# Value projections of both mixers over 512 weight columns at a time, in a two-layer encoder on one core

## The chip, the cores and the metric

The kernel runs on one core of one Trainium2 chip. The metric is the device time of one execution in microseconds (us), taken as the median of several runs. Within a core TensorE (PE in the tables; PEld is its weight load, which runs beside its matmuls), VectorE (DVE), ScalarE (ACT) and GpSimd (POOL) each work through a queue of their own in order, and wait for each other by semaphores. SyncE (SP) issues the weight transfers.

## The reference, cut to what matters

512 tokens of width 1024 pass two layers. Layer 0 joins a gated linear recurrence in both directions (4 heads of 128) with a latent attention (4 heads); layer 1 is a differential attention with 8 heads. Each is followed by a gated hidden layer of width 2816. The values that the change touches are plain projections of the normed input `h`:

```
z = h @ w_in                                       # layer 0, columns split
q_h, f_fw, f_bw, i_h, g_h, cq, ckv, kr = jnp.split(z, AB_SPLITS, axis=-1)
v = heads(i_h)                                     # 4 heads x 128 = columns 1536..2047
o_a = hgrn2_scan(q, k_fw, v, lf_fw) + flip(hgrn2_scan(flip(q), flip(k_bw), flip(v), flip(lf_bw)))
...
q, k, v = jnp.split(h @ w_in, 3, axis=-1)          # layer 1
v = v.reshape(bsz, s, DIFF_HEADS, 2 * DIFF_HEAD_DIM)   # 8 heads x 128 = columns 2048..3071
```

## The kernel before, in words

Every projection is computed in three matmuls per block of 128 input rows (`mm3`, L245): both operands are split into a high and a low part, and high x high, high x low and low x high are added up in one PSUM bank. The weights come in pieces of 128 x 1024 numbers in the order of a written list (`weight_plan`, L48): SP loads a piece (`_load`), ACT rounds it to its high part `whi`, DVE subtracts to get `wlo` (`_split`, L227 and L228). Two raw pieces and four split pieces fit at a time; a split piece is free again when TensorE has read it for the last time.

There are two forms of projection. `features` has the weights as the stationary operand and streams all 512 tokens, 256 columns (two heads) to a call, so its matmuls are 128x512; in the trace they read `mm<-oph,whi`. `values` (L293) has the tokens as the stationary operand and streams weight columns, since its result must stand with tokens on the partitions: before, a call covers 256 columns (two heads), so each matmul is 128x256 (`mm<-whi,oph`), and four token blocks x 8 input blocks x 3 make 96 of them. There are two such calls in layer 0 (at the end of `gates(0)` and `gates(1)`, L571) and four in layer 1 (at the end of `diff_inputs`, L989).

The order of TensorE's work is as the program writes it. Generators are woven: `weave` gives each thread a step count, and the thread with the smallest share done goes next. In layer 0, `gates(0)` runs by itself; then `gates(1)` is woven with the scans of heads 0 and 1 (`hgrn`, L566), and the latent projections with the scans of heads 2 and 3. A scan begins with `kk`, a sum on POOL (L575), and the matmuls `lv<-q,kk` (L579) that read it; then come seven levels, each with copies on ACT (L595, L597), products on DVE (`merge`, L649), a product on POOL (L652) and a matmul (L587). The other engines' queues are set by a scheduler, which puts `kk` behind the gate product `g` (L558) on POOL.

In layer 1 the first pair of heads gets its inputs alone (`need(0)`); then the inputs of the other pairs are woven with `diff_heads`, a pipeline over 32 units (8 heads x 4 token blocks): scores `sc`, softmax, transposition `pt`, product with the values `o`, and at a head's end a transposition back `ot`. What is left of the heads is woven with the first half of the output projection `c_out`; the last `ot` stands in its second half. Eight PSUM banks are shared by all.

Of the kernel before, what the change touches and what calls it, by code (L numbers as in the profile page):

```python
# [20 lines left out]
AF = mybir.ActivationFunctionType  # L21
# [26 lines left out]
def weight_plan():  # L48
    plan = []
    for p in range(2):  # L50
        for base in (512, 1024, 0, 2048, 1536):
            plan += [("ab_in", k, 4, base + 256 * p, 256) for k in (0, 4)]
    for c in (2560, 2816, 3072):
        plan += [("ab_in", k, 4, c, 256) for k in (0, 4)]
    plan += [("uq", k, 1, 0, 768) for k in range(3)]
    plan += [("ukv", k, 1, 0, 1024) for k in range(2)]
    for k in (0, 4):
        plan += [("ab_out", k, 4, 256 * j, 256) for j in range(4)]
    plan += ffn_plan(0)
    for hp in range(4):  # L60
        for base in (0, 1024, 2048):
            plan += [("c_in", k, 4, base + 256 * hp, 256) for k in (0, 4)]
    for k in (0, 4):
        plan += [("c_out", k, 4, 256 * j, 256) for j in range(4)]
    plan += ffn_plan(1)
    return plan
# [57 lines left out]
class Kernel:  # L124
# [108 lines left out]
    def weight(self, *key, ahead=2):  # L233
# [7 lines left out]
        hi, lo = self.splits.pop(i)  # L241
        return tuple(t[:, :kn * cn].rearrange("p (k n) -> p k n", k=kn) for t in (hi, lo))


    def mm3(self, ps, lhs, rhs, first, last):  # L245
        mm = self.nc.tensor.matmul
# [46 lines left out]
    def values(self, w, cols, xop, r):  # L293


        V = self.s4("v")
        wt = [self.weight(w, k, 4, cols, 256, ahead=a) for k, a in ((0, 2), (4, 1))]
        for b2 in range(2):
            ps = self.bank()
            for i in range(2):  # L300
                b = 2 * b2 + i
                for k in range(8):
                    self.mm3(ps[:, 256 * i:256 * i + 256], tuple(v[:, b * 128:(b + 1) * 128] for v in xop(k)),
                             tuple(v[:, k % 4, :] for v in wt[k // 4]), k == 0, k == 7)
                    if k % 4 == 3 and (i, k) != (1, 7):
                        yield
            for i in range(2):
                b = 2 * b2 + i
                self.nc.scalar.activation(V[:, b2, 256 * i:256 * i + 256], ps[:, 256 * i:256 * i + 256], AF.Copy,
                                          scale=r[:, b:b + 1])  # L310
            yield
        return V


# [218 lines left out]
    def gates(self, p, xg, st):  # L533

        nc = self.nc
        st += [dict(F=self.s4("F"), QK=self.s8("QK")) for _ in range(2)]
        for d, base in ((0, 512), (1, 1024)):
            def forget(i, ps):
                h = 2 * p + i
                if self.R is None:  # L540
                    self.R = self.spread(self.r)
                z = self.s2("z")
                nc.vector.tensor_mul(z[:], ps[:], self.R[:])
                sp = self.s2("sp")
                nc.scalar.activation(sp[:], z[:], AF.Sigmoid)
                nc.scalar.activation(z[:], z[:], AF.Sigmoid, scale=-1.0)
                f, k = st[i]["F"][:, d, :], st[i]["QK"][:, 3 * d, :]
                nc.vector.tensor_scalar(f, sp[:], self.oml[:, d, h:h + 1], self.lb[:, d, h:h + 1], ALU.mult, ALU.add)
                nc.vector.tensor_scalar_mul(k, z[:], self.omlc[:, d, h:h + 1])

            yield from self.features("ab_in", base + 256 * p, FULL, xg, forget)
        for nm, base in (("q", 0), ("g", 2048)):
            def silu(i, ps):
                z = self.s2("z")
                nc.vector.tensor_mul(z[:], ps[:], self.R[:])
                s = self.s2(nm)
                nc.scalar.activation(s[:], z[:], AF.Sigmoid)
                nc.gpsimd.tensor_mul(s[:], z[:], s[:])  # L558
                st[i][nm] = s
                if nm == "q":  # L560
                    nc.vector.tensor_mul(st[i]["QK"][:, 2, :], s[:], st[i]["F"][:, 0, :])
                    nc.vector.tensor_mul(st[i]["QK"][:, 1, :], s[:], st[i]["F"][:, 1, :])

            yield from self.features("ab_in", base + 256 * p, FULL, xg, silu)
        st[0]["V"] = st[1]["V"] = yield from self.values("ab_in", 1536 + 256 * p, xg, self.r)

    def hgrn(self, h, st, oa):


        nc = self.nc  # L570
        F, QK, V, q, g = (st[n] for n in ("F", "QK", "V", "q", "g"))  # L571
        AT = self.s8("AT")
        diag = ap(AT, 0, [[640, 4], [1, 128]])
        kk = self.s2("kk")
# [1 line left out]
        ps = self.bank("lv")  # L576
# [39 lines left out]
        for half, (ks, qs) in enumerate(((0, 2), (3, 1))):  # L616
            ps = self.bank("lv")
            t0 = 256 * (1 - half)
            for i in range(2):
                b = 2 * half + i  # L620
# [2 lines left out]
            nc.scalar.copy(AT[:, 2 * half:2 * half + 2, t0:t0 + 256],  # L623
                           ps[:].rearrange("p (b t) -> p b t", b=2))
        yield
        po = self.bank("o")
        for t in range(NB):
            for s in range(NB):
                c0 = 256 * (s % 2) + 128 * (h % 2)
# [342 lines left out]
    def diff_inputs(self, hp, xg, stats, st):  # L972

        nc = self.nc
        st += [dict(qk=self.s8("qk", F32R), kl=[self.s2("kl", F32R) for _ in range(2)]) for _ in range(2)]
        for j, base in enumerate((0, 1024)):
            todo = [] if self.R is not None else [lambda: setattr(self, "r", self.rms(stats[0], D))]

            def turn(i, ps):
                if self.R is None:  # L980
                    self.R = self.spread(self.r)
                    self.rcos, self.rsin = self.s2("rcos"), self.s2("rsin")
                    nc.vector.tensor_mul(self.rcos[:], self.R[:], self.cos)
# [5 lines left out]
        st[0]["V"] = st[1]["V"] = yield from self.values("c_in", 2048 + 256 * hp, xg, self.r)  # L989

    def diff_heads(self, sts, op, need):

# [64 lines left out]
    def layer0(self):  # L1057
        op = self.operand()
        lat = {}
        s0, s1 = [], []  # L1060
        self.R = None
        self.setup()
        xg = self.operand()
# [21 lines left out]
        next(work)  # L1085
        self.late_constants()
        drain(work)
        weave((self.gates(1, xg, s1), 42), (self.hgrn(0, s0[0], op), 13), (self.hgrn(1, s0[1], op), 17))
        scans = [self.hgrn(2, s1[0], op), self.hgrn(3, s1[1], op)]
        weave((self.latents(self.R, xg, lat), 32), (scans[0], 11), (scans[1], 11), lead=True)  # L1090
        weave((self.mla_heads(lat, op), 92), (scans[0], 27), (scans[1], 27),
# [5 lines left out]
    def layer1(self, xg, stats):  # L1097
# [5 lines left out]
        def inputs():  # L1103
            for hp in range(4):
                yield from self.diff_inputs(hp, xg, stats, st[hp])
                done.append(hp)
                yield

# [6 lines left out]
        need(0)  # L1115
        self.ended = []
        heads = self.diff_heads(st, op, need)
        weave((work, 72), (heads, 95), lead=True)
        while len(self.ended) < 4:
            next(heads)  # L1120
        weave((self.projection("c_out", [(0, 4)], op), 10), (heads, 25))
# [65 lines left out]
```

## Time and profile before

| | us |
|---|---|
| median of 3 runs (range) | 1326.63 (1326.47 to 1327.24) |
| profiled execution, its own time | 1326.59 |
| its span, first to last instruction | 1324.8 |
| TensorE busy | 1306.2 |
| DVE busy | 759.8 |
| ACT busy | 539.1 |
| POOL busy | 159.5 |

The profile gives one execution. Durations of matmuls overlap, since TensorE begins one while the one before drains; what a matmul costs is the distance between two starts, and that is read from the timeline. What a line of `mm3` does in one call or another is told apart by the names and shapes.

### The profile page before, as it was taken

Reading aid. Unit: us, or ns where it says so; the run is one execution under the profiler, and the core shown is the slowest. Engines: PE = TensorE matmul, PEld = TensorE weight load, DVE = VectorE, ACT = ScalarE, POOL = GpSimd, SP = SyncE. Lnnn points to the kernel's source line nnn. Section 1 sums busy time; section 2 is a strip of 40 time slices with the busy share of each in tenths; the row PEclk is TensorE's granted clock in tenths of the full one; section 3 lists DMA queues with packets and bytes.
Section 4 is the critical chain, followed back from the end, with each engine's and each line's share of the span. In section 5 each row is a group of like instructions: output and inputs, shape, how many; then the busy total and the mean of one; then the engine's idle time right before and its main releaser. Section 6 shows DMA issues by size and latency. Waiting matters only on the chain. (4 is left out here: it accounts for less than half of the span.)

```text
span 1324.8 us, 16816 instructions
## 1 busy us (share of the span) xinstructions
PE 1306.2 (99%) x6666; PEld 1111.7 (84%) x6666; DVE 759.8 (57%) x1196; ACT 539.1 (41%) x938; POOL 159.5 (12%) x147
## 2 busy tenths in 40 slices
PE   7999999999999999999999999999999999999997
PEld 6888988888888888888888889888788888888886
DVE  5677499645444344434467888887745534433454
ACT  6454464744322222212253566665433212322332
POOL 0322232002000000000034223120300000000002
PEclk9999999999999999999999999999999999999999
DMA  6321331112232333233232221221232233223321
GB/s 211 112 79 49 87 93 65 48 33 80 88 102 97 96 96 95 95 96 95 87 105 80 80 65 49 64 65 49 80 95 96 96 98 103 98 98 95 95 96 64
DMA packets 106675, 115.15 MB, mean 87 GB/s; under 512 B 6826, under 2 KB 98660, under 8 KB 106596
## 3 DMA queue, kind: packets, MB, share of 16 engines
q1 hardware_dynamic: 105268, 112.10, 26.8%
q10 hardware_dynamic: 1328, 1.97, 0.4%
q8 instruction: 52, 0.85, 0.3%
q14 instruction: 27, 0.22, 0.1%
HBM read 111.97 MB, written 2.10 MB: 86 GB/s over the span
## 5 line engine op out<-in xcount | busy, mean ns | idle before, releaser
L247 PE MATMUL mm<-oph,whi 128*128 128x512 f32 (+1 forms) x1320 | 520.4, 394 | 1.6 <-ACT whi L227 1.6
L249 PE MATMUL mm<-oph,wlo 128*128 128x512 f32 (+1 forms) x1320 | 513.4, 389 | 0.0
L248 PE MATMUL mm<-opl,whi 128*128 128x512 f32 (+1 forms) x1320 | 513.0, 389 | 0.0
L228 DVE TENSOR_TENSOR wlo<-raw,whi 128x1024 fp32r<-128x1024 f32 (+1 forms) x190 | 228.5, 1203 | 287.4 <-ACT whi L227 286.5
L227 ACT CAST whi<-raw 128x1024 fp32r<-128x1024 f32 (+1 forms) x190 | 195.0, 1027 | 400.8 <-PE mm L248 242.0
L249 PEld LDWEIGHTS mm<-oph,wlo 128*128 128x128 f32 x1320 | 248.4, 188 | 51.5 <-DVE wlo L228 0.2
L247 PEld LDWEIGHTS mm<-oph,whi 128*128 128x128 f32 x1320 | 248.7, 188 | 50.3 <-ACT whi L227 2.0
L248 PEld LDWEIGHTS mm<-opl,whi 128*128 128x128 f32 x1320 | 248.8, 188 | 48.9 <-DVE opl L256 0.5
L247 PE MATMUL mm<-whi,oph 128*128 128x256 f32 (+1 forms) x374 | 125.2, 335 | 0.0
L249 PE MATMUL mm<-whi,opl 128*128 128x256 f32 (+1 forms) x374 | 123.8, 331 | 0.0
L248 PE MATMUL mm<-wlo,oph 128*128 128x256 f32 (+1 forms) x374 | 123.8, 331 | 0.0
L348 POOL TENSOR_TENSOR sq<-sq,sq 128x512 f32<-128x512 f32 x24 | 34.9, 1454 | 459.8 <-ACT sq L354 459.6
L248 PEld LDWEIGHTS mm<-wlo,oph 128*128 128x128 f32 x374 | 71.0, 190 | 6.9
L247 PEld LDWEIGHTS mm<-whi,oph 128*128 128x128 f32 x374 | 70.9, 190 | 6.9
L249 PEld LDWEIGHTS mm<-whi,opl 128*128 128x128 f32 x374 | 70.9, 190 | 6.6
L704 ACT ACTIVATE p<-sc,mx 128x512 f32<-128x512 f32 x80 | 55.1, 691 | 45.2 <-DVE mx L702 40.7
L880 DVE TENSOR_TENSOR z<-mm,R 128x512 f32<-128x512 f32 x44 | 30.4, 692 | 59.7 <-PE mm L249 55.5
L255 ACT CAST oph<-u 128x512 fp32r<-128x512 f32 x44 | 27.4, 622 | 87.3 <-DVE u L887 87.3
L701 DVE TENSOR_REDUCE mx<-sc 128x1 f32<-128x512 f32 x80 | 53.2, 681 | 16.1 <-PE sc L843 13.6
L519 DVE TENSOR_TENSOR xT<-xT,mm 128x512 f32<-128x512 f32 x56 | 38.4, 685 | 34.4 <-PE mm L249 34.4
L722 PEld LDWEIGHTS o<-v,pt 128*128 128x128 f32 x384 | 49.4, 191 | 3.1
L722 PE MATMUL o<-v,pt 128*128 128x128 f32 x384 | 50.6, 274 | 0.0
(193 smaller groups left out, 1297.5 us busy)
## 6 DMA issues: line engine op xcount, KB each, us to landing
raw<-in_ffn_w_gate_dram SPq DMA_DIRECT2D x44, 512.0 KB, 3.6
raw<-in_ffn_w_up_dram SPq DMA_DIRECT2D x44, 512.0 KB, 3.6
raw<-in_ffn_w_down_dram SPq DMA_DIRECT2D x42, 512.0 KB, 3.4
raw<-in_ab_w_in_dram SPq DMA_DIRECT2D x24, 512.0 KB, 3.6
raw<-in_c_w_in_dram SPq DMA_DIRECT2D x24, 512.0 KB, 3.6
xs<-in_x_dram SPq DMA_DIRECT2D x8, 512.0 KB, 6.1
raw<-in_ab_w_out_dram SPq DMA_DIRECT2D x8, 512.0 KB, 3.4
raw<-in_c_w_out_dram SPq DMA_DIRECT2D x8, 512.0 KB, 3.4
```

The source lines that it names most:

```text
L227: self.nc.scalar.copy(h, r)
L228: self.nc.vector.tensor_sub(l, r, h.bitcast(F32))
L247: mm(ps, lhsT=lhs[0], rhs=rhs[0], start=first, stop=False)
L248: mm(ps, lhsT=lhs[0], rhs=rhs[1], start=False, stop=False)
L249: mm(ps, lhsT=lhs[1], rhs=rhs[0], start=False, stop=last)
L255: nc.scalar.copy(hi, src)
L348: self.nc.gpsimd.tensor_add(acc[0][:], acc[0][:], s[:])
L519: nc.vector.tensor_add(self.x(j), self.x(j), ps)
L701: nc.vector.reduce_max(m[:], ps, axis=AX.X)
L704: nc.scalar.activation(p[:], ps, AF.Exp, bias=m[:], scale=scale, accum_out=l)
L722: self.nc.tensor.matmul(po[:, tb * 128:(tb + 1) * 128], lhsT=pt[:, s * 128:(s + 1) * 128], rhs=V[:, s // 2, c:c + 128], start=s == 0, stop ...
L880: nc.vector.tensor_mul(z[:], ps[:], self.R[:])
```

## The change

`values` now takes 512 columns (four heads) in one call. The six calls become three: one in layer 0, columns 1536 to 2047, and two in layer 1. A weight piece holds two input blocks x 512 columns where it held four x 256, so there are as many pieces and bytes as before (12 pieces). A call goes twice over its four pieces, for two token blocks each time, and holds two PSUM banks during each pass; it yields 16 times, each time after six matmuls of 128x512. `prefetch` splits the pieces that come after the call during the second pass.

In layer 0 the call no longer stands in `gates`: `scan_values` runs ahead of `gates(1)`, in the weave with the scans of heads 0 and 1, and a scan looks its values up only at its last product. In layer 1 the call follows the inputs of head pairs 0 and 2.

```diff
 def weight_plan():
     plan = []
     for p in range(2):
-        for base in (512, 1024, 0, 2048, 1536):
+        for base in (512, 1024, 0, 2048):
             plan += [("ab_in", k, 4, base + 256 * p, 256) for k in (0, 4)]
+        if p == 0:
+            plan += [("ab_in", k, 2, 1536, 512) for k in range(0, 8, 2)]
...
+    def prefetch(self, n):
+
+        while self.n_split <= min(self.n_used + n - 1, len(self.plan) - 1):
+            self._split()
...
     def values(self, w, cols, xop, r):
...
-        V = self.s4("v")
-        wt = [self.weight(w, k, 4, cols, 256, ahead=a) for k, a in ((0, 2), (4, 1))]
+        V = [self.s4("v"), self.s4("v")]
+        wt = []
         for b2 in range(2):
-            ps = self.bank()
-            for i in range(2):
-                b = 2 * b2 + i
-                for k in range(8):
-                    self.mm3(ps[:, 256 * i:256 * i + 256], tuple(v[:, b * 128:(b + 1) * 128] for v in xop(k)),
-                             tuple(v[:, k % 4, :] for v in wt[k // 4]), k == 0, k == 7)
-                    if k % 4 == 3 and (i, k) != (1, 7):
-                        yield
...
+            pss = [self.bank(), self.bank()]
+            for j in range(4):
+                if b2 == 0:
+                    wt.append(self.weight(w, 2 * j, 2, cols, 512, ahead=min(2, 3 - j)))
+                else:
+                    self.prefetch(j - 1)
+                for i in range(2):
+                    b = 2 * b2 + i
+                    for k in (2 * j, 2 * j + 1):
+                        self.mm3(pss[i][:], tuple(v[:, b * 128:(b + 1) * 128] for v in xop(k)),
+                                 tuple(v[:, k % 2, :] for v in wt[j]), k == 0, k == 7)
+                    if j == 3:
+                        for p in range(2):
+                            self.nc.scalar.activation(V[p][:, b2, 256 * i:256 * i + 256],
+                                                      pss[i][:, 256 * p:256 * p + 256], AF.Copy, scale=r[:, b:b + 1])
+                    yield
         return V
...
-        st[0]["V"] = st[1]["V"] = yield from self.values("ab_in", 1536 + 256 * p, xg, self.r)
+
+    def scan_values(self, xg, *sts):
+
+        V = yield from self.values("ab_in", 1536, xg, self.r)
+        for st, v in zip(sts, V):
+            for s in st:
+                s["V"] = v
...
-        weave((self.gates(1, xg, s1), 42), (self.hgrn(0, s0[0], op), 13), (self.hgrn(1, s0[1], op), 17))
+        weave((self.chain(self.scan_values(xg, s0, s1), self.gates(1, xg, s1)), 48),
+              (self.hgrn(0, s0[0], op), 13), (self.hgrn(1, s0[1], op), 17))
...
                 yield from self.diff_inputs(hp, xg, stats, st[hp])
+                if hp % 2 == 0:
+                    V = yield from self.values("c_in", 2048 + 256 * hp, xg, self.r)
+                for s in st[hp]:
+                    s["V"] = V[hp % 2]
                 done.append(hp)
                 yield
...
-        weave((work, 72), (heads, 95), lead=True)
+        weave((work, 68), (heads, 95), lead=True)
```

The first place is TensorE's queue where the scans of heads 0 and 1 begin. Before, the 96 value matmuls stand between the last gate feature and the features with which the scans are woven; these are the rows from the last value matmul on (`lv<-q,kk` are the scans' first matmuls):

```order
L249 MATMUL mm_629<-whi_531,opl_235 128x256
L247 MATMUL mm_684<-oph_108,whi_572 128x512
L248 MATMUL mm_684<-opl_109,whi_572 128x512
L249 MATMUL mm_684<-oph_108,wlo_573 128x512
L247 MATMUL mm_684<-oph_108,whi_572 128x512
L248 MATMUL mm_684<-opl_109,whi_572 128x512
L249 MATMUL mm_684<-oph_108,wlo_573 128x512
L579 MATMUL lv_707<-q_475,kk_705 128x128 x4
L579 MATMUL lv_716<-q_494,kk_714 128x128 x4
L247 MATMUL mm_684<-oph_120,whi_572 128x512
```

With the change the rows from the last gate feature (`mm_500`) on are these:

```order
L258 MATMUL mm_500<-oph_234,wlo_456 128x512
L256 MATMUL mm_573<-whi_501,oph_108 128x512
L257 MATMUL mm_573<-wlo_502,oph_108 128x512
L258 MATMUL mm_573<-whi_501,opl_109 128x512
L256 MATMUL mm_573<-whi_501,oph_108 128x512
L257 MATMUL mm_573<-wlo_502,oph_108 128x512
L258 MATMUL mm_573<-whi_501,opl_109 128x512
L599 MATMUL lv_590<-q_475,kk_588 128x128 x4
L599 MATMUL lv_599<-q_494,kk_597 128x128 x4
L256 MATMUL mm_574<-whi_501,oph_108 128x512
```

Between the last gate feature and the first `lv` now stand six matmuls, where 96 value matmuls and six features stood. At the scans of heads 2 and 3 it is the same: six features of the latent projections stand there now, where the second call's 96 value matmuls stood ahead of them. POOL's queue around the first `kk` is as it was, with `kk` for both heads behind the first `g`:

```order
L572 TENSOR_TENSOR q_475<-z_473,q_475 128x512
L572 TENSOR_TENSOR q_494<-z_492,q_494 128x512
L572 TENSOR_TENSOR g_551<-z_549,g_551 128x512
L595 TENSOR_TENSOR kk_588<-QK_130 128x512
L595 TENSOR_TENSOR kk_597<-QK_132 128x512
L572 TENSOR_TENSOR g_568<-z_566,g_568 128x512
```

At the second pair of scans POOL's queue before has both `g` and a norm's power `rt` ahead of the `kk`:

```order
L558 TENSOR_TENSOR g_1222<-z_1220,g_1222 128x512
L558 TENSOR_TENSOR g_1258<-z_1256,g_1258 128x512
L321 TENSOR_TENSOR rt_1305<-ms_1303,mhalf 128x4
L575 TENSOR_TENSOR kk_1435<-QK_681 128x512
L575 TENSOR_TENSOR kk_1444<-QK_683 128x512
```

and with the change one `g`:

```order
L334 TENSOR_TENSOR rt_1200<-ms_1198,mhalf 128x4
L572 TENSOR_TENSOR q_1212<-z_1210,q_1212 128x512
L572 TENSOR_TENSOR q_1231<-z_1229,q_1231 128x512
L572 TENSOR_TENSOR g_1297<-z_1295,g_1297 128x512
L595 TENSOR_TENSOR kk_1339<-QK_829 128x512
L595 TENSOR_TENSOR kk_1348<-QK_831 128x512
L572 TENSOR_TENSOR g_1314<-z_1312,g_1314 128x512
```

The second pair now stands in the same pattern as the first: one `g`, both `kk`, the other `g`.

## Rows read from the trace of the kernel before

**Rows 1.** The page: span, and busy time of each engine.
```profile
span 1324.8 us, 16816 instructions
PE 1306.2 (99%) x6666; PEld 1111.7 (84%) x6666; DVE 759.8 (57%) x1196; ACT 539.1 (41%) x938; POOL 159.5 (12%) x147
```
**Rows 2.** All of TensorE's waits: for whom, us in total, times, longest.
```profile
PE pv L428 <- DMA ra<-in_norm_attn_dram: 5.3, 1, 5.3
PE mm L247 <- ACT whi L227: 1.6, 1, 1.6
PE ot L369 <- DVE on L360: 1.2, 1, 1.2
PE sc L1005 <- ACT pt L714: 1.1, 1, 1.1
PE ss L340 <- POOL sq L348: 1.0, 2, 0.8
PE pt L712 <- ACT p L704: 0.8, 1, 0.8
```
**Rows 3.** Timeline of TensorE, gate features then values: start us, us, line, operation.
```profile
52.79 0.39 PE L247 MATMUL mm<-oph,whi 128*128 128x512 f32 x1
...
59.59 0.28 PE L247 MATMUL mm<-whi,oph 128*128 128x256 f32 x1
...
60.06 0.28 PE L248 MATMUL mm<-wlo,oph 128*128 128x256 f32 x1
...
67.86 0.28 PE L247 MATMUL mm<-whi,oph 128*128 128x256 f32 x1
```
**Rows 4.** The page's groups: the low part of a weight piece; busy us, mean ns.
```profile
L228 DVE TENSOR_TENSOR wlo<-raw,whi 128x1024 fp32r<-128x1024 f32 (+1 forms) x190 | 228.5, 1203 | 287.4 <-ACT whi L227 286.5
```
**Rows 5.** Tile v: duration ns min/median/max of its copies out of PSUM.
```profile
L309 ACT ACTIVATE v<-mm,rt x24: 466/476/519, 66.9 to 882.2; 128x256 f32<-128x256 f32 x24
```
**Rows 6.** Timeline of POOL, then of DVE, where the first scans begin.
```profile
58.50 1.29 POOL L558 TENSOR_TENSOR g<-z,g 128x512 f32<-128x512 f32 x1 [5.38 <-ACT g L557]
59.75 3.54 POOL L575 TENSOR_TENSOR kk<-QK 128x512 f32<-128x512 f32 x2
60.69 1.45 DVE L228 TENSOR_TENSOR wlo<-raw,whi 128x1024 fp32r<-128x1024 f32 x1 [0.21 <-ACT whi L227]
63.33 1.77 DVE L649 TENSOR_TENSOR QK<-QK,F 128x512 f32<-128x512 f32 x1 [1.19 <-POOL kk L575]
```
**Rows 7.** Line L575: duration ns min/median/max of the four kk.
```profile
L575 POOL TENSOR_TENSOR kk<-QK x4: 1287/1297/2281, 59.8 to 147.3; 128x512 f32<-128x512 f32 x4
```
**Rows 8.** Timeline of TensorE, the first two lv<-q,kk and the matmul behind.
```profile
72.49 1.95 PE L579 MATMUL lv<-q,kk 128*128 128x128 f32 x16
74.19 0.48 PE L247 MATMUL mm<-oph,whi 128*128 128x512 f32 x1
```
**Rows 9.** Windows of layer 1's mixer: us, busy of PE, PEld, DVE, ACT, POOL, PEclk, DMA, GB/s.
```profile
734.00:755.00 21.00, 21.00 (x100) 17.43 (x100) 18.72 (x40) 11.66 (x26) 3.23 (x3) 1.00 0.24 77
755.00:773.00 18.00, 18.00 (x145) 17.47 (x144) 15.89 (x38) 11.59 (x26) 8.89 (x10) 1.00 0.10 30
773.00:811.00 38.00, 38.00 (x211) 32.22 (x210) 33.24 (x86) 24.03 (x65) 5.89 (x5) 1.00 0.23 70
```
**Rows 10.** DVE groups of 720 to 882 us: the three long ones of a unit.
```profile
L701 DVE TENSOR_REDUCE mx<-sc 128x1 f32<-128x512 f32 x48 | 31.8, 680 | 1.7 <-PE sc L1006 1.7
L1012 DVE SCALAR_TENSOR_TENSOR p<-p,l,p 128x512 f32<-128x512 f32 x24 | 18.9, 790 | 0.4
```
**Rows 11.** Timeline of TensorE, POOL and DVE around the last ot of layer 1.
```profile
925.37 1.05 PE L722 MATMUL o<-v,pt 128*128 128x128 f32 x8
...
931.76 0.66 PE L369 MATMUL ot<-cst,on 128*128 128x128 f32 x4 [1.25 <-DVE on L360]
928.83 1.95 POOL L321 TENSOR_TENSOR rt<-ms,mhalf 128x4 f32<-128x4 f32 x1 [11.24 <-DVE ms L319]
928.69 1.22 DVE L228 TENSOR_TENSOR wlo<-raw,whi 128x1024 fp32r<-128x1024 f32 x1
```

More of the change, by code (lines that the diff above doesn't have):

```diff
@@ L60, in weight_plan @@
     for hp in range(4):
-        for base in (0, 1024, 2048):
+        for base in (0, 1024):
             plan += [("c_in", k, 4, base + 256 * hp, 256) for k in (0, 4)]
+        if hp % 2 == 0:
+            plan += [("c_in", k, 2, 2048 + 256 * hp, 512) for k in range(0, 8, 2)]
     for k in (0, 4):
@@ L293, in values @@
     def values(self, w, cols, xop, r):
-        V = self.s4("v")
-        wt = [self.weight(w, k, 4, cols, 256, ahead=a) for k, a in ((0, 2), (4, 1))]
+        V = [self.s4("v"), self.s4("v")]
+        wt = []
         for b2 in range(2):
-            ps = self.bank()
-            for i in range(2):
-                b = 2 * b2 + i
-                for k in range(8):
-                    self.mm3(ps[:, 256 * i:256 * i + 256], tuple(v[:, b * 128:(b + 1) * 128] for v in xop(k)),
-                             tuple(v[:, k % 4, :] for v in wt[k // 4]), k == 0, k == 7)
-                    if k % 4 == 3 and (i, k) != (1, 7):
-                        yield
[L307 to L311, printed above, removed]
+            pss = [self.bank(), self.bank()]
[14 more added lines that the diff above has]
+                    yield
         return V
@@ L535, in gates @@
         nc = self.nc
-        st += [dict(F=self.s4("F"), QK=self.s8("QK")) for _ in range(2)]
+        for s in st:
+            s.update(F=self.s4("F"), QK=self.s8("QK"))
         for d, base in ((0, 512), (1, 1024)):
@@ L564, in gates @@
             yield from self.features("ab_in", base + 256 * p, FULL, xg, silu)
-        st[0]["V"] = st[1]["V"] = yield from self.values("ab_in", 1536 + 256 * p, xg, self.r)
+    def scan_values(self, xg, *sts):
+        V = yield from self.values("ab_in", 1536, xg, self.r)
+        for st, v in zip(sts, V):
+            for s in st:
+                s["V"] = v
     def hgrn(self, h, st, oa):
         nc = self.nc
-        F, QK, V, q, g = (st[n] for n in ("F", "QK", "V", "q", "g"))
+        F, QK, q, g = (st[n] for n in ("F", "QK", "q", "g"))
         AT = self.s8("AT")
@@ L625, in hgrn @@
         yield
-        po = self.bank("o")
+        po, V = self.bank("o"), st["V"]
         for t in range(NB):
@@ L988, in diff_inputs @@
             yield from self.later(self.features("c_in", base + 256 * hp, FULL, xg, turn), *todo, steps=3)
-        st[0]["V"] = st[1]["V"] = yield from self.values("c_in", 2048 + 256 * hp, xg, self.r)
     def diff_heads(self, sts, op, need):
@@ L1059, in layer0 @@
         lat = {}
-        s0, s1 = [], []
+        s0, s1 = [{}, {}], [{}, {}]
         self.R = None
@@ L1105, in inputs @@
                 yield from self.diff_inputs(hp, xg, stats, st[hp])
+                if hp % 2 == 0:
+                    V = yield from self.values("c_in", 2048 + 256 * hp, xg, self.r)
+                for s in st[hp]:
+                    s["V"] = V[hp % 2]
                 done.append(hp)
```

## The prediction, on record before the changed kernel ran

> **What bounds the kernel now.** I read the page's busy times first, then TensorE's waits, then its timeline around a value call. TensorE is busy 1306.2 of 1324.8 us [rows 1], and all its waits together are some 11 us, the first 5.3 at the start [rows 2]. So the time is TensorE's issue time plus a handful of waits: a change counts by how it alters the distance between matmul starts, and by the waits that it adds or takes. A busy sum of matmuls says little here, since each drains while the next begins (0.39 us long, 0.23 apart); the reader is to look at starts. In the timeline 30 matmuls of 128x512 lie between 52.79 and 59.59: 6.80 / 30 = 0.2267 us each. 65 matmuls of 128x256 lie between 60.06 and 67.86: 7.80 / 65 = 0.1200 us each [rows 3]. Half the columns cost more than half the time; 2 x 0.1200 - 0.2267 = 0.0133 us is what one matmul costs beside its columns.
>
> **The change, part by part.** *The matmuls.* Six calls of 96 matmuls of 128x256 go: 576 x 0.1200 = 69.12 us. Three calls of 96 matmuls of 128x512 come: 288 x 0.2267 = 65.28 us. The difference is -3.84 us, -1.28 for layer 0's pair of calls and -2.56 for layer 1's four. All of it is on TensorE's path.
>
> The Trainium skill (TensorE: Matmul & The Clock Gate, Back-to-back issue gap) gives a warm gap of columns / 2.4 GHz + 2.5 ns for a single stream, so a fixed part of 2.5 ns. By that 288 matmuls fewer would save 288 x 0.0025 = 0.7 us, an estimate, and not 3.84; it also says that weight loads change the spacing in a real stream. The rows of this trace give 13.3 ns, and they decide.
>
> *Weights and copies.* There are 12 pieces of 128x1024 before and after, so ACT's and DVE's splits (1.203 us each on DVE [rows 4]) and the bytes are the same, and the copies out of PSUM stay 24 of 128x256 (0.476 us [rows 5]). I cost these at nothing; the cover is that they lie on ACT and DVE. What is new is that four pieces are held to the second pass, while only four fit: the piece behind the call in layer 0 can be split when TensorE has left the first piece in the second pass, after which it has 36 more matmuls (36 x 0.2267 = 8.2 us) and scan levels to do. ACT's cast and DVE's subtraction need some 2.3 us of that; the scan's products stand ahead of it on DVE, but those run from 63.33 on [rows 6], well ahead of TensorE. Without the cover it would cost up to those 2.3 us; I take 0.
>
> *The scan's start, first pair.* Here something is lost. The first `lv<-q,kk` waited for nothing before, since 96 value matmuls stood ahead of it. With the change it stands six matmuls behind the last gate feature, and POOL's queue is unchanged: `g`, both `kk`, the other `g`. Up to this point every queue is the same, so the times of before hold. The call begins at 59.59 [rows 3]; six matmuls later TensorE is at 59.59 + 6 x 0.2267 = 60.95. The `kk` run from 59.75 to 63.29 [rows 6]; with the median of 1.297 [rows 7] the first ends at 61.05, the second at 63.29. The first `lv` thus starts at about 61.09 (0.14 late). A pair of them takes 74.19 - 72.49 = 1.70 us [rows 8], so 0.85 each, and the second would start at 61.94, but waits until 63.33, as the product on DVE did for the same `kk` [rows 6]. That is 1.39 us, and 1.53 with the first. TensorE's queue is in order: the rest of the value call stands behind it and waits too. Bounds: 0.6 (both `kk` at the median: 61.05 + 1.30 = 62.35) and 1.6.
>
> The second `kk` lasted 2.28 us against 1.30 [rows 7], while DVE's subtraction from two SBUF inputs ran from 60.69 for 1.45 us [rows 6]. The Trainium skill (SBUF — State Buffer, Who interferes with whom) has a DVE instruction with two SBUF inputs and a reading GpSimd instruction lock each other out. The trace agrees, by about a microsecond. The subtraction stands at the same place in the change, so by that rule the long `kk` stays; without it the sum would be 0.9 us lower at each pair.
>
> *The scan's start, second pair.* Before, 96 value matmuls of 0.12 us covered it; now six latent features do, and POOL has the pattern of the first pair: one `g`, both `kk`. Measured from the end of the last gate feature, T, the first pair had its `g` at T - 1.09 (58.50 against 59.59) and the second `kk` done at T + 3.70. If DVE gives `z` for that `g` as early here, the wait is again 1.5 us. DVE has a head's output and a weight piece ahead of it here, which can make it up to 0.7 later (2.2). With both `kk` at 1.30 they end at T + 0.20 + 2.60 = T + 2.80, and the waits are 0.14 and 0.45, 0.6 in all. I take 1.5, by the first pair as the nearest rows.
>
> *Scans.* Their steps are spread over a longer stretch (48 steps of 1.36 us where it was 42), so DVE and ACT have more room; I take 0.
>
> *Layer 1.* Head pairs 1 and 2 now get their features one after the other, with no value call between. Two waits of before, 1.1 and 0.8 us [rows 2], lie in this mixer at the third pair; they are jitter in a pipeline of eight PSUM banks, and the like will come elsewhere. I take the same sum; bounds: -1.9 (both go), and 5 more, by the second rival.
>
> *The last `ot`.* Before, 18 matmuls stand between the last `o` and the last `ot`, now 12: 1.36 us less cover, where TensorE already waits 1.25 us [rows 11]. Against it: before, the norm's power on POOL took 1.95 us beside a weight subtraction of 1.22 [rows 11], and in the change's queue that subtraction stands ahead of the norm. Without the overlap the power is shorter by up to those 1.22. The two about cancel: 0, bounds -1.2 and 1.4.
>
> *Sum.* -3.84 + 1.53 + 1.5 + 0 = -0.8 us on the profiled execution's 1326.59 (span 1324.8 and 1.8 around it), which lies 0.04 below the median: **1325.8 us**.
>
> **The rivals.** *The `kk` stay covered.* If POOL had both sums before TensorE came, the change is worth its whole 3.84 us: 1322.8. For it: POOL sat idle 5.38 us ahead of `g` [rows 6], and the inputs of `kk` were there by then. Against it: its queue is in order, and in the change's queue `kk` still stand behind `g`. Chance 0.12.
>
> *DVE's arrears in layer 1 (slower).* The mechanism: during the features of a head pair DVE turns queries and keys and serves the softmax; 18.72 of 21 us and 33.24 of 38 us are busy [rows 9]. Between pairs 1 and 2 lay a value stretch of 18 us with 15.89 busy and three units. A unit's long instructions are 2 x 0.68 + 0.79 [rows 10], 2.15, some 2.5 with the small ones, so three make 7.5; four half pieces of the next pair are some 2.7; what is left, 5.7, was arrears from the features before. That stretch goes. The features of pair 2 have 38 - 33.24 = 4.8 us to spare, so up to 0.9 us is late even if nothing is lost in order, and all 5.7 when no spare can be used. Then scores hold their banks longer and TensorE waits: 1325.8 + 5.7 = 1331.5. It decides from about 3.5 us of waits on. Against it: pair 2 had no wait of TensorE in 38 us, and a unit's result is wanted only three units later. Chance 0.2.
>
> *The columns alone count.* If a matmul of 512 cost twice one of 256, nothing is gained and 3.0 us of waits stay: 1329.6. Rows 3 speak against it in plain numbers; chance 0.03. By the page's 2.5 ns it would be 1325.8 + 3.1 = 1328.9, which falls in the same chance.
>
> **How the numbers follow.** The forecast has 0.65. A difference under 0.2% (2.65 us) can't be told from none, so "same" is 1323.97 to 1329.28. The forecast's own range is 1323.3 (its `kk` waits at their low ends, or layer 1's waits gone) to 1328.6 (the high ends and a longer tail); some 0.1 of its chance falls below 1323.97 and 0.03 above 1329.28. Faster: 0.12 + 0.1 = 0.22. Slower: 0.2 of the second rival, of which 0.17 reaches over 1329.28, with 0.03 of the third and 0.03: 0.23. Same: 0.55. The range takes in most of the first rival and most of the second: 1322.7 to 1331.0.
>
> **What would show it.** Right: value matmuls 0.2267 us apart; a wait of `lv` on POOL's `kk` of about 1.4 us at 62 us and again at the second scans, rows that the waits of before don't have; layer 1's waits of TensorE still about 2 us; the wait of `ot` near 1.3. Wrong: no wait on `kk` (first rival), several waits of `sc` or `pt` on ACT between 740 and 870 us with DVE over 95% busy (second), or a wait of `mm` on `wlo` behind a value call, which would be the cover that I counted as safe.

## The result and the profile after

The change is slower. It takes 1344.32 us (median of 4 runs, 1342.80 to 1345.66) against 1326.93 (1326.47 to 1327.50) for the kernel before, run beside it: a ratio of 1.0130, with a 95% interval of 1.0117 to 1.0143, or about 17.4 us. The forecast was 1325.8, the range ended at 1331.0.

The page of the profiled execution, against [rows 1]: TensorE has 288 instructions fewer, DVE and ACT the same number, and the span is 17.5 us longer.

```profile
span 1342.3 us, 16249 instructions
PE 1308.8 (98%) x6378; PEld 1097.4 (82%) x6378; DVE 761.7 (57%) x1196; ACT 539.5 (40%) x938; POOL 159.8 (12%) x147
```

The view of TensorE's waits, against [rows 2] (line, what it waited for: us in total, times, longest):

```profile
PE pv L441 <- DMA ra<-in_norm_attn_dram: 5.6, 1, 5.6
PE sc L1024 <- DVE on L373: 3.6, 1, 3.6
PE sc L1024 <- ACT pt L734: 3.5, 2, 2.6
PE lv L599 <- POOL kk L595: 2.4, 3, 1.1
PE ot L382 <- DVE on L373: 2.0, 2, 1.3
...
PE o L742 <- ACT pt L734: 1.7, 1, 1.7
PE pt L732 <- ACT p L724: 1.3, 2, 0.8
...
PE sc L1024 <- DVE ra L680: 1.0, 1, 1.0
PE mm L256 <- ACT p L724: 0.9, 1, 0.9
PE pt L732 <- DVE on L373: 0.8, 1, 0.8
...
```

The waits at `lv` were forecast. New and not forecast in this number are those at `sc`, `pt` and `o`, and that of `mm` on `p`: all lie in layer 1's mixer. One of the two at `ot`, 0.7 us at 240 us, is new as well. Where I sum TensorE's losses below, I add up how much later each matmul starts than the median distance for its shape and the shape before it; by that sum TensorE loses some 20 us more in this execution than in the one before, which fits the 17.5 us of span and the 3.84 us of matmuls saved.

The first scans, against [rows 3, 6, 7] (timeline: start us, duration, engine, line, operation):

```profile
60.08 0.39 PE L256 MATMUL mm<-whi,oph 128*128 128x512 f32 x1
60.24 3.51 POOL L595 TENSOR_TENSOR kk<-QK 128x512 f32<-128x512 f32 x2
60.31 0.39 PE L257 MATMUL mm<-wlo,oph 128*128 128x512 f32 x1
...
61.60 1.16 PE L599 MATMUL lv<-q,kk 128*128 128x128 f32 x8
...
63.80 0.94 PE L599 MATMUL lv<-q,kk 128*128 128x128 f32 x6 [1.05 <-POOL kk L595]
```

Value matmuls of 512 columns start 0.23 us apart, and the second `lv` waits until both `kk` are done.

Layer 1's mixer in windows (from:to, us, busy of PE, PEld, DVE, ACT, POOL, granted clock, DMA, GB/s): the first value call, the features of pair 1, those of pair 2, and the second value call, each from its first matmul on.

```profile
719.35:741.11 21.76, 21.76 (x97) 18.02 (x96) 11.66 (x17) 9.45 (x17) 9.66 (x10) 1.00 0.32 97
741.11:770.65 29.54, 29.54 (x141) 24.64 (x140) 22.62 (x51) 16.83 (x35) 4.21 (x3) 1.00 0.23 72
770.65:814.42 43.77, 38.48 (x209) 31.87 (x208) 40.90 (x91) 24.16 (x57) 13.79 (x15) 1.00 0.21 61
814.42:853.79 39.37, 34.85 (x172) 28.49 (x170) 25.04 (x62) 21.34 (x60) 9.80 (x10) 0.96 0.14 41
```

The same view of the kernel before for its first value call:

```profile
715.72:727.23 11.51, 11.51 (x97) 11.51 (x96) 8.27 (x13) 5.35 (x10) 8.11 (x9) 1.00 0.26 79
```

Two things are to be seen. While the first value call runs, the program starts no head, and DVE is idle for 10 us (21.76 - 11.66) where it was idle for 3 (11.51 - 8.27). And in the features of pair 2 DVE is busy 93% of the time, where it was 87% [rows 9], and TensorE, which had no gap there, 88%: that stretch takes 43.77 us.

By place, TensorE's losses in this mixer (delays over 0.12 us each) are 6.2 us in the features of pair 2, 6.4 in the second value call, and 4.7 from 881 to 908 us, at the end of pair 3's features and the start of the output projection, which now follows them with no value call between. The kernel before lost 2.3 us in the same mixer, in two waits.

How one wait comes about shows in the timeline:

```profile
777.53 0.40 PE L1025 MATMUL sc<-kl,qk 128*128 128x512 f32 x1
777.89 0.69 DVE L682 TENSOR_TENSOR ra<-ra,sw 128x512 f32<-128x512 f32 x1 [0.68 <-POOL sw L681]
778.62 1.26 ACT L691 CAST qk<-ra 64x512 fp32r<-64x512 f32 x2 [2.84 <-DVE ra L682]
...
779.90 0.59 ACT L734 COPY pt<-pt 128x512 f32<-128x512 f32 x1
...
780.54 0.50 PE L1024 MATMUL sc<-qk 128*128 128x512 f32 x1 [2.61 <-ACT pt L734]
```

ACT's queue is in order. A copy of rotated keys stands there for 2.84 us because DVE's `ra` is late; the copy of `pt` behind it, whose input had long been ready, frees its PSUM bank late; the next score needs that bank. The profile names ACT, but `ra` on DVE is behind it, and this `ra` itself waited 0.68 us for POOL's product `sw`, which could begin only after a shuffle on DVE.

### The profile page after: what moved, and what is told of

Its sections match the earlier page's. It is cut to its first block, busy times and chain, and to the rows that moved or that the text cites. A ratio compares the mean times of both kernels' runs of the same rounds, so it can differ in the third digit from the quotient of the medians.

```text
span 1342.3 us, 16249 instructions
## 1 busy us (share of the span) xinstructions
PE 1308.8 (98%) x6378; PEld 1097.4 (82%) x6378; DVE 761.7 (57%) x1196; ACT 539.5 (40%) x938; POOL 159.8 (12%) x147
## 5 line engine op out<-in xcount | busy, mean ns | idle before, releaser
L256 PE MATMUL mm<-whi,oph 128*128 128x512 f32 (+1 forms) x278 | 108.8, 391 | 0.0
L258 PE MATMUL mm<-whi,opl 128*128 128x512 f32 (+1 forms) x278 | 107.5, 387 | 0.0
L257 PE MATMUL mm<-wlo,oph 128*128 128x512 f32 (+1 forms) x278 | 107.4, 386 | 0.0
L258 PEld LDWEIGHTS mm<-whi,opl 128*128 128x128 f32 x278 | 52.5, 189 | 10.7
L256 PEld LDWEIGHTS mm<-whi,oph 128*128 128x128 f32 x278 | 52.5, 189 | 10.4 <-ACT p L724 0.4
L257 PEld LDWEIGHTS mm<-wlo,oph 128*128 128x128 f32 x278 | 52.6, 189 | 10.0
```

What stands on the lines that cost most here:

```text
L256: mm(ps, lhsT=lhs[0], rhs=rhs[0], start=first, stop=False)
L257: mm(ps, lhsT=lhs[0], rhs=rhs[1], start=False, stop=False)
L258: mm(ps, lhsT=lhs[1], rhs=rhs[0], start=False, stop=last)
```

## The experiments

Each was run beside the kernel before on the same chip. Times are medians, and the interval behind each is the 95% one of its ratio. Two experiments can come from different chips; the medians of the kernel before beside them lie within 0.4 us of each other.

**One layer at a time.** e1 has the change in layer 0 alone, e2 in layer 1 alone: the other layer's plan, calls and weave are those of before.

> Only layer 0 has its values over 512 columns; layer 1 is as before. Against 1326.9 us before. Theory A (the loss is DVE's arrears in layer 1): layer 0 gives 1.28 us of matmuls back and pays 2.9 us of waits for kk that the trace of the change shows, +1.6, so 1328.5 (1327.5 to 1329.5). Theory B (the wider calls themselves cost, by two PSUM banks held for each call or by four weight pieces in place of two, in both layers): half of the 17.4 us and more, 1334 or above.

> Only layer 1 has its values over 512 columns, with the change's order (features of pairs 1 and 2 in a row) and its weave of 68 to 95; layer 0 is as before. Theory A: all of the loss but the 1.6 us of layer 0, so 1326.9 + 17.4 - 1.6 = 1342.7 us (1341 to 1344), with the stalls of TensorE in 770 to 920 us as in the change. Theory B: 1336 or less, the rest in layer 0.

e1: 1330.69 us against 1326.78 (1.0018 to 1.0039, +3.9). e2: 1341.73 against the same (1.0097 to 1.0127, +14.9). The losses add up to the change's within their spread. Layer 1 is the larger by far; layer 0 costs some 2 us more than expected.

**The order alone.** e3 is e2 with two narrow calls in place of each wide one.

```diff
-                    V = yield from self.values("c_in", 2048 + 256 * hp, xg, self.r)
+                    V = []
+                    for p in (hp, hp + 1):
+                        V.append((yield from self.values256("c_in", 2048 + 256 * p, xg, self.r)))
```

> As e2, but each value call of 512 columns is two calls of 256 columns, one behind the other, with one PSUM bank at a time and weight pieces as before: the change's order without its wide matmuls. Theory A (the order makes the arrears): e2's time and 2.56 us for the narrow matmuls, 1345 us (1342 to 1347). Rival C (the wide call holds two banks, and that starves the scores): the loss goes, 1326 to 1330.

1338.85 us (1.0074 to 1.0108, +12.1). So the order does most of the harm without any wide matmul, and the rival is out as the whole cause. But 1345 was expected, and neither theory's range was met: with the 2.56 us of its matmuls, the wide call must cost some 5 us of its own (1341.73 + 2.56 - 1338.85).

**Less work for DVE.** e4 is e2, e9 the kernel before, both without the sine half of the rotation.

```diff
-                self.stacked(self.rope(ps[:], self.rcos[:], self.rsin[:]), qk[:, 2 * j:2 * j + 2, :], kl if j else None)
+                a = self.s2("ra")
+                nc.vector.tensor_mul(a[:], ps[:], self.rcos[:])
+                self.stacked(a, qk[:, 2 * j:2 * j + 2, :], kl if j else None)
```

> As e2, but the rotation of layer 1's queries and keys leaves out its sine half: DVE's shuffle (0.74 us) and sum (0.69 us) and POOL's product go, 1.4 us of DVE for each of the four row blocks of a pair, 5.7 us a pair. TensorE's work is the same. Theory A (TensorE waits because DVE is behind): the waits of layer 1 go almost all, 1324.3 (before less 2.56) to 1328 us. Rival D (TensorE waits for an order of banks, for ACT or for the clock, and DVE is only busy beside it): 1338 us or more.

> The kernel before, with the sine half of layer 1's rotation left out as in e4: the control for e4. Theory A (in the change DVE is behind beside the features and TensorE waits for it; before it is behind too, but the value calls let it catch up before TensorE feels it): at most the 2 us of waits that before has in this mixer, 1324 to 1327 us. If it falls by 5 us or more, then e4's gain is not a sign of DVE's arrears in the change.

e4: 1332.87 us (1.0030 to 1.0060), 8.9 less than e2. e9: 1325.71 against 1327.15 (0.9981 to 1.0000), 1.4 less. The same work is worth 9 us behind the change's order and hardly anything before: DVE's arrears are the larger part of the loss. e4 fell between the two expectations, so they are not all of it. The edit also takes a product off POOL, so it does not test DVE's load alone; but DVE stood idle for that product for only 1.6 us in 745 to 811 us of the change (the group `ra<-ra,sw` further down). How the arrears build up, worked out from the traces as the time from the end of a unit's first score to DVE's first look at it, in us (units counted from 0):

| unit | 2 | 3 | 4 | 5 | 6 | 7 | 9 | 12 | 13 | 14 | 15 | 23 | 24 |
|---|---|---|---|---|---|---|---|---|---|---|---|---|---|
| before | 5.6 | 4.2 | 2.2 | 4.8 | 2.2 | 1.6 | 0.4 | 0.7 | 1.5 | 4.2 | 5.1 | 4.4 | 0.4 |
| e2 | 6.1 | 4.7 | 2.1 | 8.8 | 5.3 | 0.8 | 4.4 | 4.4 | 3.5 | 0.0 | 0.0 | 6.9 | 7.3 |
| e4 | 2.0 | 1.6 | 1.3 | 0.9 | 2.0 | 1.4 | 2.5 | 4.3 | 3.5 | 0.0 | 0.0 | 5.9 | 6.1 |

DVE is 5 us behind in the kernel before as well, without harm. The difference begins at unit 5, where before had a value call and the change has the next features. At units 12 and 13, beside the second wide call, e4 is as late as e2; behind them it still has one wait of 3.6 us and slower matmuls. It also loses 3.2 us at the end of the features of pair 3 (units 23 and 24).

**The second bank.** e13 lets the wide call work off one row block at a time, with one PSUM bank; e16 does so for the second call only.

```diff
-        for b2 in range(2):
-            pss = [self.bank(), self.bank()]
+        for b in range(4):
+            ps = self.bank()
```

> As e2 (after's order, layer 1 alone, 1341.7 us), but the wide value call works off one row block after the other, with one PSUM bank held at a time in place of two. Theory C' (of e2's loss some 5 us are the second bank: e3, with one bank and narrow matmuls, was 2.9 us faster than e2 where 2.6 slower was expected): e3's 1338.9 less 2.6, 1336.3 us, and the wait of 3.8 us at 819 us falls to about 1.5. If the second bank does not matter: 1341 us or more.

> As e2 (1341.7 us), but the second wide call, which has units beside it, holds one PSUM bank at a time, row block after row block; the first call stays as in e2, so that the wait for a weight piece of e13 does not come (2.7 us and a slower stretch behind it, 4.5 in all). Theory C'': the second bank of that call costs 4 to 5 us once DVE is behind: 1337 us (1336 to 1338.5). If not: 1340 or more.

> e16 with the sine half of layer 1's rotation left out, as in e4 (1332.9 us). If DVE's arrears and the second bank together are layer 1's loss, e4's one large wait left in 750 to 850 us (3.8 us at 811 and the slower matmuls behind it) goes too: 1327 to 1329 us, with what is left at the end of features 3 (3.1 us at 887). If e4's rest has another cause: 1331 us or more.

e13: 1340.95 us (1.0087 to 1.0118). The large wait fell as expected, but the time did not: the first call now goes through its weight pieces twice as fast and waits 2.4 us for one on DVE, with matmuls at the lower clock behind it. e16 leaves the first call alone: 1337.45 (1.0062 to 1.0090), 4.3 less than e2, as expected. Both edits also move the copies of the values and the splits of the next pieces, so they test the form of the call and not the bank alone. In the change the place looks like this:

```profile
822.55 0.40 PE L1025 MATMUL sc<-kl,qk 128*128 128x512 f32 x1
826.57 0.50 PE L1024 MATMUL sc<-qk 128*128 128x512 f32 x1 [3.62 <-DVE on L373]
826.90 0.57 PE L1025 MATMUL sc<-kl,qk 128*128 128x512 f32 x1
827.27 0.63 PE L256 MATMUL mm<-whi,oph 128*128 128x512 f32 x1
827.70 0.63 PE L257 MATMUL mm<-wlo,oph 128*128 128x512 f32 x1
```

A score waits for the bank of a finished head, and behind it the matmuls stand 0.43 us apart for a while. In e16 TensorE's longest wait there is shorter, and the matmuls behind it keep their distance:

```profile
823.60 0.50 PE L254 MATMUL mm<-whi,oph 128*128 128x512 f32 x1 [1.36 <-DVE on L417]
823.93 0.40 PE L255 MATMUL mm<-wlo,oph 128*128 128x512 f32 x1
824.17 0.40 PE L256 MATMUL mm<-whi,opl 128*128 128x512 f32 x1
```

The windows of this place, e2's first and then e16's, show a granted clock of 0.57 and 1.00:

```profile
821.00:829.00 8.00, 6.16 (x19) 5.25 (x20) 4.46 (x12) 2.63 (x7) 0.87 (x1) 0.57 0.00 0
818.00:830.00 12.00, 10.02 (x54) 8.02 (x53) 9.28 (x26) 6.87 (x17) 4.15 (x5) 1.00 0.00 0
```

So the wait in e16's execution is 2.3 us shorter (1.36 against 3.62), and some 3 us of slower matmuls behind it are gone too; the 4.3 us hold both.

e17, with the sine half left out too: 1328.15 us (0.9998 to 1.0017), as expected, 9.3 less than e16. With both taken away, 1.1 us is left over the kernel before. Against e9, which has the same rotation, it is 2.4, and since the wide matmuls give 2.56 back, some 5 us of loss are still there. The trace has them at 884 to 890 us, at the end of the features of pair 3: waits of 1.76 and 1.07 us and slower matmuls behind them. That place was not tested by itself.

**Dealing the units out otherwise.** Same instructions as e2, other places for the 32 softmax units or the parts. In all four a pair is ready when its features are there. e10 also puts four steps of the output projection ahead of its first unit. The edit shown is e5's; e6 and e10 have other numbers and begin in the first value call, and e7 keeps 68 to 95 and moves the second value call ahead of the features of pair 2.

```diff
-        weave((work, 68), (heads, 95), lead=True)
+        for n, h in [(17, 14), (17, 13), (17, 36), (17, 18)]:
+            weave((part(work, n), n), (heads, h), lead=True)
```

> As e2 (layer 1 alone, wide calls, features of pairs 1 and 2 in a row, first value call alone), but the softmax units are dealt out unevenly: 3 to 4 beside the features of pair 1, 4 beside those of pair 2, 10 beside the second value call, 6 beside pair 3, where e2 had 5, 7, 5 and 7; and a pair counts as ready when its features are there. Same instructions, same banks. Theory A (DVE cannot serve 5 to 7 units beside a pair's features, about 19 us of its own for 21.8 us of matmuls and 2.9 us a unit, and TensorE waits for it): the waits go, 1324.3 to 1328 us. Rival C (the wide value call holds two banks and takes them from the units): more units beside it make it worse, 1335 us or more.

> As e5, and the heads start ahead of the first value call too, which gets 5 units; then 3, 4, 7 and 5 beside the features of pair 1, of pair 2, the second value call and the features of pair 3. Theory A: at or a little below e5, 1322 to 1327 us, since 22 us of DVE's rest are used. Rival C: 1335 us or more.

> As e2, with the weave of 68 to 95 throughout, but the second wide value call stands between the features of pairs 1 and 2, and pairs 2 and 3 come in a row: units 5, 6, 3 to 4 and 7 beside features 1, values, features 2, features 3. Theory A: no arrears at the first two, some at the last (7 units beside features, as in e2, 4 us of waits): 1326 to 1330 us. Rival E (any two features in a row cost the same, wherever): 1338 us or more.

> Layer 1 alone, wide calls, order features 0, values 0 and 1, features 1, features 2, values 2 and 3, features 3 as in e2. The units begin five steps into the first value call, and are dealt out 5, 2, 3, 8, 6 over the parts, with no unit of a pair right behind its features, where e6 waited 15 us for POOL's copies; the output projection has four steps ahead of its first unit. Theory A' (the change lets the first value call run alone, 22 us with DVE idle, so that the same DVE work has 10 us less of TensorE's time to lie beside; given back, the waits go): 1323 to 1329 us. If the loss is in the wide calls or in features in a row as such: 1336 us or more.

e5: 1340.01 us (1.0083 to 1.0113). The time lies where rival C had it. But units 8 to 18, beside the second value call, had next to no delay (0 to 1.2 us), so more units there do not make it worse by themselves. Three to four units beside features are still too many: unit 7 waited 10.1 us for DVE, and the stalls stand where it does, at the start of the second value call. Whether that call's two banks add to them was not told apart. My number was wrong. e6: 1347.47 (1.0140 to 1.0170), a miss with a new reason: units of a pair came right behind its features and waited for POOL's copies. e7: 1340.10 (1.0081 to 1.0114), a miss too, with the same wait at pair 2. The waits of e6 between 700 and 910 us:

```profile
PE sc L1059 <- POOL qk L730: 11.3, 2, 6.2
PE sc L1060 <- POOL kl L731: 3.0, 3, 1.2
PE o L777 <- ACT v L334: 2.3, 2, 2.0
...
```

A value call behind each pair's features, as before had it, thus also gives these copies time. e10 heeds it and starts the heads inside the first value call: 1333.62 (1.0038 to 1.0068), 8.1 less than e2. TensorE lost nothing new up to 800 us, through the features of pairs 1 and 2 with five units; then the arrears came due, 5.2 us of stalls and slower matmuls at 800 to 808 us, again at the start of the second value call. That is half a confirmation: my expectation ended at 1329, and the lead of the output projection is in it too.

**Half the width.** e11 and e14 have narrow calls for pairs 0 and 1 as before and one wide call for pairs 2 and 3; e14 also spreads the units, and e15 adds e12's layer 0. All three have e10's lead of the output projection.

> Layer 1 alone: pairs 0 and 1 as before (a narrow value call behind each pair's features), pairs 2 and 3 with one wide call behind the features of pair 2, and pair 3's features right ahead of the output projection, which has four steps ahead of its first unit. Weave 72 to 95 as before. Half of the wide matmuls, 1.28 us less. Theory A': the first value call is short again and pairs 1 and 2 have values between them, so no new waits up to 850 us; 1325.5 to 1328.5 us. If a wide call as such costs: 1331 us or more.

> Layer 1 alone: pairs 0 and 1 with a narrow value call behind each pair's features, pairs 2 and 3 with one wide call between their features. Units are dealt to the parts by what DVE has free there: 2 in the first value call (from its fifth step of eight), 3 to 4 beside features 1, 2 beside values 1, 5 beside features 2, 7 beside the wide call, 4 beside features 3, 8 beside the output projection after a lead of four steps. Theory A' (DVE's capacity by stretch decides): no arrears anywhere, so -1.28 for the matmuls and up to -2 for layer 1's waits of before: 1323.5 to 1326 us. If the wide call itself costs: 1330 us or more, as e11.

> e14's layer 1 and e12's layer 0 (wide calls, kk added early). If the two parts add: e14 less 0.6 us (e12 against before), 1323 to 1325.5 us, at or just under before; if the layers do not add, the difference shows at layer 1's waits.

e11: 1330.52 us (1.0015 to 1.0038), 2 us over its range: nothing new up to 850 us as expected, then two waits of 2.4 and 2.1 us at 879 and 895 us, where the output projection follows the features of pair 3 directly. e14: 1332.86 (1.0030 to 1.0055), a miss: a wait of 2.4 us at 811, where units 12 and 13 were 4 and 6 us behind as the wide call took its two banks, and 1.2 us for POOL's copies. e15: 1331.58 (1.0023 to 1.0049); the layers add, though the range, built on e14's, was missed.

**Layer 0.** e8 puts four steps of TensorE's work ahead of each pair of scans. e12 adds `kk` earlier on POOL.

```diff
             yield from self.features("ab_in", base + 256 * p, FULL, xg, forget)
+        for s in st:
+            s["kk"] = self.s2("kk")
+            nc.gpsimd.tensor_add(s["kk"][:], s["QK"][:, 0, :], s["QK"][:, 3, :])
```

> As e1 (layer 0 alone), but four steps of the wide value call (24 matmuls) stand ahead of the first scans' start, and four steps of the latent features ahead of the second's, so that POOL has both sums kk done. If the kk waits are all of layer 0's loss: e1 less 2.9 us, 1327.8 us, or 1326.5 with the wait for ot at 240 us gone as well. If the waits only come back later in the scans: 1329 to 1331 us as e1.

> As e1 (layer 0 alone), but POOL adds kk right behind the forget gates' features, ahead of the work for q and g, so that it is there when the scan begins; TensorE's order is e1's. If the three waits for kk are layer 0's loss: e1's 1330.7 less 2.9 us, 1327.8 us (1326.5 to 1328.5). If they only hide another wait of the scans: 1329.5 us or more.

e8: 1336.64 us (1.0058 to 1.0088). A miss: the `kk` waits went, but the shift brought a wait for a small weight piece of the latent projections at 207 us, which stood in DVE's queue behind four scan products (2.5 us) and the rotation of the latent keys:

```profile
PE mm L256 <- DVE wlo L223: 5.1, 1, 5.1
```

e12: 1326.54 us (0.9987 to 1.0005), 4.2 less than e1. No `lv` waits any more (the wait of `ot` at 237 us stays, 0.9 us):

```profile
61.80 1.94 PE L621 MATMUL lv<-q,kk 128*128 128x128 f32 x16
62.12 1.79 POOL L595 TENSOR_TENSOR g<-z,g 128x512 f32<-128x512 f32 x1 [1.47 <-ACT g L594]
```

**A version faster than before?** e18 has e12's layer 0 and, in layer 1, the narrow calls of before with the heads begun in the first one.

> Layer 0 as in e12 (wide calls, kk early). Layer 1 with the narrow calls and the order of the kernel before, but the heads begin in the first value call (2 units there) and the features get 3 to 5 units in place of 5 to 7. Theory A': before's two waits at 853 and 868 us (2.2 us) go and nothing comes: 1323.5 to 1325.5 us, under before. If before's layer 1 has no room that a spread can use: 1326.5 us, as e12.

1326.70 us against 1327.06 (0.9990 to 1.0007): no difference that can be told. The two waits of before went, and three of 0.6 to 0.9 us came. None of the kernels that do the whole work is measurably faster than the kernel before.

## Why the prediction was wrong, step by step

*Matmuls, -3.84.* Right: 0.23 us apart, and no wait for a value piece.

*The `kk` waits, 1.53 and 1.5.* Right. By the starts, TensorE lost 1.4 us at the first pair and 1.7 at the second, 3.0 in all, and e12 shows that these waits are real losses. Layer 0 was still dearer than the sum of both terms (+1.75): e1 measured +3.9. About 1.0 of it is a second wait of `ot` for DVE's `on` at 240 us, which before did not have and I did not look for; the other 1.2 lie within e1's interval.

*The last `ot`, 0.* Right, with the reason given: the power on POOL no longer ran beside the weight subtraction and took 1.01 us, where it took 1.95 [rows 11], and TensorE waited 1.28 where it waited 1.25.

```profile
944.24 1.05 PE L742 MATMUL o<-v,pt 128*128 128x128 f32 x8
947.24 1.01 POOL L334 TENSOR_TENSOR rt<-ms,mhalf 128x4 f32<-128x4 f32 x1 [8.20 <-DVE ms L332]
949.31 0.63 PE L382 MATMUL ot<-cst,on 128*128 128x128 f32 x4 [1.28 <-DVE on L373]
```

*Layer 1, "I take the same sum".* This step failed. The waits that I called jitter were the edge of an engine at its limit: e2 lost 14.9 us where the term was 0 and the matmuls gave 2.56 back. The mechanism is the second rival's, to which I gave 0.2 and a price of 5.7 us. In its own place the price held: the features of pair 2 took 43.77 us against 38.04, 5.7 more. That the two agree to the tenth is luck, since the units beside them differ. The price stopped there, and the second value call and the end of pair 3's features lost 6.4 and 4.7 us more. The price left out three things:

- The first value call. It went from 96 matmuls of 0.12 us to 96 of 0.2267, from 11.5 to 21.8 us, and no head runs beside it. DVE's work of layer 1 is the same but has some 7 us less of TensorE's time to lie beside (10 us idle against 3). I had priced only the value stretch between pairs 1 and 2. e10, which gives DVE units to work on there, takes 8.1 of the 14.9 us away, though it deals out the other parts differently as well.
- What a unit adds beside features. DVE's groups in 745 to 811 us of the change (a line ends with DVE's idle time before the group and what ended it):

```profile
L721 DVE TENSOR_REDUCE mx<-sc 128x1 f32<-128x512 f32 x22 | 14.6, 678 | 1.9 <-PE sc L1025 1.9
L1031 DVE SCALAR_TENSOR_TENSOR p<-p,l,p 128x512 f32<-128x512 f32 x11 | 9.9, 897 | 0.1
L225 DVE TENSOR_TENSOR wlo<-raw,whi 128x512 fp32r<-128x512 f32 x8 | 6.0, 749 | 0.0
L693 DVE TENSOR_TENSOR qk<-ra,qk 64x512 fp32r<-64x512 f32 x8 | 5.5, 687 | 0.3
L679 DVE STREAM_SHUFFLE sw<-mm 128x512 f32<-128x512 f32 x7 | 5.1, 735 | 0.0
L682 DVE TENSOR_TENSOR ra<-ra,sw 128x512 f32<-128x512 f32 x6 | 4.1, 687 | 1.6 <-POOL sw L681 1.6
L680 DVE TENSOR_TENSOR ra<-mm,rcos 128x512 f32<-128x512 f32 x6 | 4.1, 675 | 0.0
L693 DVE TENSOR_TENSOR kl<-ra,qk 64x512 fp32r<-64x512 f32 x4 | 3.8, 952 | 0.1
L232 DVE TENSOR_TENSOR wlo<-raw,whi 128x1024 fp32r<-128x1024 f32 x3 | 3.6, 1216 | 0.0
...
```

  A row block of queries costs DVE 0.74 + 0.68 + 0.69 + 2 x 0.69 = 3.5 us, one of keys 4.0; a pair has two of each, 15, and four weight pieces of 1.2: some 20 us beside 21.8 us of feature matmuls. A unit costs DVE 2 x 0.68 + 0.90 and some 0.7 of small instructions, 3 us, and TensorE about 2 (an estimate from its 4 matmuls of 512 columns, 4 transpositions and 4 products). So two pairs' features with 12 units ask 76 us of DVE and give it 68: 8 us of arrears by this estimate. The trace does not show the 8 as such: of the 73.3 us that both pairs took, DVE was busy for 63.5, since it had little to do while the first units began and the last work fell behind the window. Before, the value call between the pairs took up arrears, 5.7 us by the prediction's reckoning. DVE's mean share (57% of the span in both pages) shows none of this.
- The form of the wide call, most likely its second PSUM bank: 4.3 us (e2 against e16), slower matmuls behind the wait included. I had weighed what the call costs TensorE, not that it keeps a second of the eight banks just when scores and a head's output hold theirs longest.

Of the second item one part is contention. The subtraction `kl<-ra,qk` of pair 1 took 0.95 us on average and the same subtraction for queries, `qk<-ra,qk`, 0.69; the keys' copies on POOL run beside the first and nothing on POOL beside the second. The Trainium skill (SBUF — State Buffer, Who interferes with whom) has a DVE instruction with two SBUF inputs lock out a reading GpSimd instruction and the other way round. The trace agrees with it: 0.27 us for each of four, 1.1 us for pair 1. The kernel before has it as well (0.68 to 1.09 us for its keys), so it is part of what a pair's features ask of DVE in both kernels, not of the difference.

What stays open: the loss of 14.9 us splits into 12.1 by order (e3), 4.3 by the form of the wide call (e16) and -2.56 by the matmuls, 13.8 in all; the rest lies within the intervals. How much of the 12.1 belongs to the lonely first call and how much to features in a row was not told apart, since each cure moved both; nor was the loss at the end of pair 3's features. And I could not turn the account into a faster kernel: e5, e7 and e14 were all expected at or under 1330 us and came out 6 to 13 us slower than before.

## What to carry to other kernels

Before merging calls, ask which stretches the small calls gave to the engine that is behind: a matmul stretch in which nothing else may run is idle time taken from DVE, and a short call between two heavy stretches may be what keeps TensorE from noticing DVE. Judge that engine by stretch (its work there against the time there), not by its share of the span, and price a wait that you call jitter by what an engine at 90% does when it gets several us less. A wider call also holds more PSUM; count the banks at the moment when they are held longest.

## What the runs showed of the hardware that was not expected

Behind some waits TensorE's matmuls ran at the lower of its two clock levels (1.2 in place of 2.4 GHz). In the change, after the waits of 0.90 and 3.62 us at 822 to 826 us, 128x512 matmuls started 0.427 us apart from 827.27 to 829.83 in place of 0.2267, and the granted clock of the second value call is 0.96; e16 with 1.36 us there kept its distance. It is no fixed price: after the 2.6 us at 780 us the change ran on at full clock, while e2 had four such matmuls behind the same wait. So a wait can cost more than its length, here some 1.3 us. It also blurs comparisons: by the starts, slower matmuls cost e2's profiled execution some 6 us in three stretches (778 to 781, 823 to 829 and 901 to 904 us), that of e4 3.4 in two, that of the change 1.7 in one, and that of e16 1.9 in one. Some 3 of e4's 8.9 us may be the clock's in this way.
